# Half of a token gather issued between the router's turns and logits, and two row loads of the last norm moved

## The chip, the cores and the metric

The kernel runs on one core of a Trainium2 chip. The metric is the device time of one execution in microseconds, as the median of several runs. Three runs of the kernel before gave 711.48, 712.3 and 713.32 us, so the median is 712.3 us.

## What is computed

One decoder layer on 256 tokens of width 2048. Three token mixers (sparse attention, stick-breaking attention, forgetting attention) run on the same input, and their outputs go through one output projection and a layer norm. A mixture of experts follows, with a second layer norm:

```python
h = layer_norm(ALPHA * h + mix, ln1_g, ln1_b)
# experts: top-1 of 4 groups, then the top 2 of the 4 experts in that group
hid = silu(xt @ wg) * (xt @ wu)          # 16 experts, 2048 -> 256
y = y + (hid * gate_column) @ wd          # 256 -> 2048
h = layer_norm(ALPHA * h + y, ln2_g, ln2_b)
```

All of it is float32. The change touches the part from the first layer norm to the second.

## The kernel before, in words

**Engines and order.** TensorE's instructions run in the order in which they are written, through the whole kernel (`manual_schedule`, from line 150 on). For VectorE, ScalarE and GpSimd a planner sets most of the order up to `order.__enter__()` (line 1176); from there, within the last block of the output projection, their order is the written one too. SyncE issues the large loads in order, each as soon as its slot is free. GpSimd issues a few small loads itself (`nc.gpsimd.dma_start`).

**Tokens and halves.** The 256 tokens are two halves `t` of 128 partitions. `vt` holds the rows, `zh` and `zl` their normalised values in two parts (hi and lo) whose sum is the float32 value. The columns are 16 blocks `k` of 128.

**The router.** The last 512 columns of the output projection are finished for half 0 first, then for half 1 (`mix1`). For half 1 the row sums, the turns (`row_turn`, TensorE transposes by a matmul with `ident`), the copies of these to SBUF by ScalarE (`row_copy`), the router's logits (`row_logits`, 20 columns), the choice of experts on VectorE (`pick`, `choose`), the counting of places (a matmul with `ut`, line 1296) and the one-hots (`place`, `fill_hots`) follow each other. Half 0 has been through all of this before. `keep_warm(n)` issues n matmuls of ones into a bank that nobody reads.

**The gather.** `S0[:, t, :]` is a one-hot matrix from tokens of half t to 4 x 64 slots of the first group's experts. `gather` computes the slots' inputs with column blocks k on the partitions. A PSUM bank holds two blocks k and k + 1 of 256 slots each. For each block TensorE issues four matmuls into the bank: hi and lo of half 0, then hi and lo of half 1 (lines 908 and 909). Then ScalarE or VectorE writes the bank to `xg` with the first norm's gain and bias (`rows_out`). The first call gathers four blocks, the next four, and so on, with `gate_up_part` between.

**PSUM.** The eight banks are named: `pj` has 2, `s` has 3, `t` has 2, `o` has 1. A new tile of a name waits until the readers of that bank's last tile are done.

**The experts.** Four groups g, each with four experts in two planes `pl`. For a group, `gate_up` multiplies the slots by 16 pieces of weights of 1 MB (line 972), `hidden` and `turn` make the hidden values, the next group's gather follows, and then `down` multiplies by 8 pieces (line 1000). It does so in two rounds `c` = 0 and 2; a round has four `down`s, each into a bank of `s`, which ScalarE (L1002) and then VectorE (L1003) split into hi and lo, and two `combine`s (line 1014) that add the results into `vt` (L1015). The weight pieces go through 11 slots in turn.

**Rows of the second norm.** `lng` and `gb` hold the second norm's gain and a five-row matrix of gain and bias parts. `norm_parts(gb, h)` makes one half (1024 columns) of `gb`: a load of five rows by GpSimd (L1037) into the single buffer `raw5`, and three VectorE steps (L1038, L1039, L1040) that use the signs in `part`. In group 1 GpSimd loads `lng`, broadcasts it and makes `part` by two selects. In group 2 `norm_parts` is called for both halves, one after the other, ahead of the first round of `down`s. `gb` and `lng` are read in group 3 and by the second norm.

Of the kernel before, what the change touches and what calls it, by code (L numbers as in the profile page):

```python
# [12 lines left out]
F32 = mybir.dt.float32  # L13
# [5 lines left out]
ALU = mybir.AluOpType  # L19
# [4 lines left out]
P = 128  # L24
T = 256
# [15 lines left out]
def kernel(  # L41
# [4 lines left out]
    nc = tc.nc  # L46
    V, A, G, PE = nc.vector, nc.scalar, nc.gpsimd, nc.tensor
# [78 lines left out]
    def ps_proj():  # L126
        return psp.tile([P, 512], F32, name="pj", bufs=2)

    def ps_s():
        return psp.tile([P, 512], F32, name="s", bufs=3)  # L130

    def ps_t():
        return psp.tile([P, 512], F32, name="t", bufs=2)
# [1 line left out]
    def ps_o():  # L135
        return psp.tile([P, 512], F32, name="o", bufs=1)

    def keep_warm(n):

        w = ps_t()  # L140
        for _ in range(n):
            PE.matmul(w[:, 0:P], ones, ones, start=True, stop=True)

# [36 lines left out]
    with tc.tile_pool(name="pa", bufs=1) as pa, \  # L180
# [45 lines left out]
        start = tc.manual_schedule(engines={mybir.EngineType.DVE, mybir.EngineType.Activation})  # L226
# [17 lines left out]
        for q in range(4):  # L244
            for j, k0 in product(range(3), (q * 4, q * 4 + 2)) if q else ((0, 0), (1, 0), (2, 0), (0, 2), (1, 2), (2, 2)):
                if k0 == q * 4:
                    if q % 2 == 0:
                        parts[j] = [t.rearrange("p (a b) -> p a b", a=8) for t in parts_tile()]
                    h, l = [t[:, q % 2 * 4:q % 2 * 4 + 4, :] for t in parts[j]]
# [7 lines left out]
                h, l = parts[j]  # L257
                for k in (k0, k0 + 1):
# [10 lines left out]
                        compare_op=ALU.is_ge, fill=0.0)  # L269
        G.affine_select(out=blkm, in_=blkm, pattern=[[16, 8]], base=15, channel_multiplier=-1,  # L270
                        compare_op=ALU.is_ge, fill=0.0)
# [142 lines left out]
        def decay_turn():  # L414
            cps = ps_t()
            for t in range(2):
# [10 lines left out]
                        channel_multiplier=1, compare_op=ALU.is_ge, fill=FAR)  # L427
# [454 lines left out]
    zh, zl = by_t(hi_t), by_t(lo_t)  # L882
# [13 lines left out]
    def fill_hots(S, g, t):  # L896
        V.tensor_tensor(S[:, t, :].rearrange("p (e s) -> p e s", e=4),
                        pm[:, t, 4 * g:4 * g + 4][:, :, None].to_broadcast([P, 4, CAP]),
                        sif[:, None, 0:CAP].to_broadcast([P, 4, CAP]), op=ALU.is_equal)

    def gather(S, xg, k0=0, k1=KT, engs="AV"):

        for n, k in enumerate(range(k0, k1, 2)):
            ps = (ps_t, ps_s)[k // 2 % 2]()
            for j in range(2):
                ks = slice((k + j) * P, (k + j + 1) * P)
                for t in range(2):
                    PE.matmul(ps[:, j * T:j * T + T], zh[:, t, ks], S[:, t, :], start=t == 0, stop=False)
                    PE.matmul(ps[:, j * T:j * T + T], zl[:, t, ks], S[:, t, :], start=False, stop=t == 1)
            rows_out(ps, xg, k, engs[n % len(engs)])  # L910


# [115 lines left out]
    eps2 = pb.tile([P, 1], F32, name="eps2")  # L1028
    V.memset(eps2, EPS / (ALPHA * ALPHA))

    part = pb.tile([P, 2], F32, name="part")
    V.memset(part, 1.0)

    def norm_parts(gb, h):
        hs_ = slice(h * 1024, h * 1024 + 1024)
        raw = praw.tile([P, 1024], F32, name="raw5")[0:5, :]
        nc.gpsimd.dma_start(raw, ln2r[:, hs_])  # L1037
        V.tensor_copy(gb[0:5, hs_], raw)  # L1038
        V.tensor_scalar(raw, raw, part[0:5, 1:2], None, op0=ALU.mult)  # L1039
        V.scalar_tensor_tensor(gb[0:5, hs_], gb[0:5, hs_], part[0:5, 0:1], raw, op0=ALU.mult, op1=ALU.add)  # L1040
# [35 lines left out]
    with ExitStack() as rows:  # L1076
# [20 lines left out]
        def row_turn(t, c, js=range(4)):  # L1097
            tp = ps_t()
            for i, j in enumerate(js):
                PE.transpose(tp[:, i * P:i * P + P], vt[:, t, c * 512 + j * P:c * 512 + j * P + P], ident)  # L1100
            return tp

        def row_copy(tp, n=4):
            vT = pb2.tile([P, 4, P], F32, name="vT")
            A.activation(vT[:, 0:n, :].rearrange("p a b -> p (a b)"), tp[:, 0:n * P], AF.Copy)
            return vT

        def row_logits(vT, t, c, js=range(4)):
            for i, j in enumerate(js):
                PE.matmul(lgp[t][:, 0:20], vT[:, i, :], gw[:, c * 4 + j, 0:20],  # L1110
                          start=c + j == 0, stop=c + j == 6)
# [34 lines left out]
        def n_lo(t, c):  # L1146
            V.tensor_tensor(zl[:, t, cols[c]], vt[:, t, cols[c]], zh[:, t, cols[c]].bitcast(F32), op=ALU.subtract)
# [125 lines left out]
        row_sums(mm[1], 1, 3, range(1))  # L1273
        mix1(3, range(4), range(1, 2))
        tpa = row_turn(1, 3, range(2))
        n_lo(0, 2)
        row_sums(mm[2], 1, 3, range(1, 2))
        vTa = row_copy(tpa, 2)
        tpb = row_turn(1, 3, range(2, 4))
        row_var(1)  # L1280
        vTb = row_copy(tpb, 2)
        row_scale(1)
        row_logits(vTa, 1, 3, range(2))
        row_logits(vTb, 1, 3, range(2, 4))
        n_lo(0, 3)
        logit_mean(1)
        row_shift(1)
# [4 lines left out]
                n_norm(1, c, "A")  # L1292
        pick(1)
        choose(1)
        keep_warm(6)
        PE.matmul(pp[1][:, 0:16], ut, A2[:, 1, :], start=False, stop=True)
        keep_warm(3)
        n_lo(1, 0)
        place(1)
        fill_hots(S0, 0, 1)  # L1300
        xg = slot_rows()
        gu = ps_proj()
        n_lo(1, 1)
        n_norm(1, 2)
        gather(S0, xg, 0, 4, "A")
# [57 lines left out]
    for g in range(NG):  # L1363
        if g:
            gu = gate_up(xg, g, 0)
        gs = gates(S, g)
        C = back(S)
        hs = [hidden(gu, gs[:, 0:1])]
        S_next = one_hots(g + 1) if g + 1 < NG else None
        gu = ps_proj()  # L1370
        for kq in range(4):
            gate_up_part(gu, xg, g, 1, kq)
            if kq == 2 and g + 1 == NG:
                hT = [turn(hs[0])]
        if g + 1 < NG:
            hT = [turn(hs[0])]
        hs.append(hidden(gu, gs[:, 1:2]))
        res = None
        if g + 1 == NG:

            A.preload_act_table_set("natural_log_exp_and_others")
            res = [xs_tile() for _ in range(2)]
        if g + 1 < NG:
            S = S_next
            xg = slot_rows()
            gather(S, xg)
            hT.append(turn(hs[1]))
        if g == 1:
            nc.gpsimd.dma_start(lng[0:1, :], ln2r[0:1, :])  # L1389
            G.partition_broadcast(lng, lng[0:1, :], channels=P)  # L1390
            gb = xgp.tile([P, D], F32R, name="lnb")
            G.affine_select(out=part[:, 0:1], in_=part[:, 0:1], pattern=[[0, 1]], base=2, channel_multiplier=-1,
                            compare_op=ALU.is_ge, fill=-1.0)
            G.affine_select(out=part[:, 1:2], in_=part[:, 1:2], pattern=[[0, 1]], base=-3, channel_multiplier=1,
                            compare_op=ALU.is_ge, fill=0.0)
        if g == 2:
            norm_parts(gb, 0)
            norm_parts(gb, 1)

        for c in (0, 2):  # L1400
            parts = [slots["o"]().bitcast(F32R).rearrange("p (l i n) -> p l i n", l=2, i=2) for _ in range(2)]
            if len(hT) == 1:
                down(g, 0, 0, hT[0], parts[0])
                hT.append(turn(hs[1]))
                down(g, 1, 0, hT[0], parts[1])
                down(g, 0, 1, hT[1], parts[0])
                down(g, 1, 1, hT[1], parts[1])
            else:
                for i, pl in product(range(2), range(2)):
                    down(g, c + i, pl, hT[pl], parts[i])  # L1410
                    if g + 1 == NG:
                        gained(res, pl, i)
            for i in range(2):
                combine(c + i, C, parts[i], res)
# [102 lines left out]
```

## Time and profile before

| | |
|---|---|
| runs | 711.48, 712.3, 713.32 us (median 712.3) |
| the profiled execution's own time | 713.84 us |
| its span | 712.1 us |
| mean granted clock of TensorE | 0.981 |
| TensorE busy | 686.2 us, 96% of the span |
| VectorE busy | 418.0 us, 59% |
| ScalarE busy | 306.9 us, 43% |
| GpSimd busy | 91.7 us, 13% |

All positions below are microseconds from the start of the span of the profiled execution. The execution's own time is 1.7 us longer than its span. A matmul's shown time includes a tail that overlaps the next one, so the rate is read from starts. One matmul of float32 operands is shown as two instructions. "Idle before" in brackets is the engine's idle time just ahead of an instruction and what ended it.

### The profile page before, as it was taken

What the parts mean: (1) busy time and instruction counts of PE and PEld (TensorE: products, weight loads), DVE (VectorE), ACT (ScalarE), POOL (GpSimd) and SP (SyncE); (2) the same over time, 40 slices, a digit from 0 to 9 for tenths busy, and PEclk for the clock granted to TensorE, in tenths of its full rate; (3) what the DMA queues carried; (4) which work ended last, traced back from release to release, by engine and by line L of the source; (5) the groups of instructions that cost most, each with busy time, mean ns of one, the idle gap of its engine ahead of it and who ended that gap; (6) DMA issues with size and microseconds to landing.
All of it is one profiled execution on the core that took longest, in us unless ns stands there. A gap on an engine that the chain in (4) does not pass through costs nothing. (4 is left out here: it accounts for less than half of the span.)

```text
span 712.1 us, 11149 instructions
## 1 busy us (share of the span) xinstructions
PE 686.2 (96%) x4327; PEld 511.4 (72%) x4327; DVE 418.0 (59%) x859; ACT 306.9 (43%) x616; POOL 91.7 (13%) x128
## 2 busy tenths in 40 slices
PE   6999999999999999999999999999999999699994
PEld 6999998887789997999788889646435443443353
DVE  4768665978648976677858436474511421451186
ACT  5444555767656774567755322522201200310120
POOL 3200101454420134210020000002000000000000
PEclk9899999999999999999999999999999999989997
DMA  8964554232233355453587517489999999989923
GB/s 296 332 217 159 200 186 179 110 119 85 94 119 119 133 185 186 173 182 119 188 345 296 179 61 267 202 357 419 420 391 421 422 420 422 418 328 373 422 91 122
DMA packets 29519, 173.70 MB, mean 244 GB/s; under 512 B 4080, under 2 KB 4104, under 8 KB 10002
## 3 DMA queue, kind: packets, MB, share of 16 engines
q1 hardware_dynamic: 28192, 170.75, 62.3%
q10 hardware_dynamic: 1172, 2.12, 1.0%
q8 instruction: 36, 0.59, 0.3%
q14 instruction: 23, 0.19, 0.1%
q0 software_dynamic: 96, 0.05, 0.0%
HBM read 170.81 MB, written 2.11 MB: 243 GB/s over the span
## 5 line engine op out<-in xcount | busy, mean ns | idle before, releaser
L92 DVE TENSOR_TENSOR hl<-raw,hl 128x1024 fp32r<-128x1024 f32 x98 | 119.0, 1232 | 40.8 <-ACT hl L91 40.1
L91 ACT ACTIVATE hl<-raw 128x1024 fp32r<-128x1024 f32 x98 | 102.2, 1054 | 47.3 <-PE pj L215 14.0
L190 PE MATMUL pj<-hi_t,hl 128*128 128x256 f32 x384 | 109.3, 285 | 3.9 <-DVE hl L252 3.9
L188 PE MATMUL pj<-hi_t,hl 128*128 128x256 f32 x384 | 112.2, 292 | 0.1
L189 PE MATMUL pj<-lo_t,hl 128*128 128x256 f32 x384 | 109.1, 284 | 0.1
L190 PEld LDWEIGHTS pj<-hi_t,hl 128*128 128x128 f32 x384 | 73.8, 192 | 4.4 <-DVE hl L252 4.4
L188 PEld LDWEIGHTS pj<-hi_t,hl 128*128 128x128 f32 x384 | 73.9, 193 | 2.6 <-issue 1.7
L189 PEld LDWEIGHTS pj<-lo_t,hl 128*128 128x128 f32 x384 | 73.9, 192 | 0.6 <-DVE lo_t L256 0.4
L972 PE MATMUL pj<-raw,xs 128*64 128x512 f32 x256 | 70.7, 594 | 0.0
L972 PEld LDWEIGHTS pj<-raw,xs 128*64 128x64 f32 x256 | 21.9, 137 | 34.5 <-issue 32.3
L1002 ACT ACTIVATE ohl<-s 128x512 fp32r<-128x512 f32 x32 | 19.1, 597 | 63.2 <-PE s L1000 63.2
L972 PE MATMUL pj<-hl,xs 128*64 128x512 f32 x144 | 46.0, 594 | 0.0
L1003 DVE TENSOR_TENSOR ohl<-s,ohl 128x512 fp32r<-128x512 f32 x32 | 21.9, 688 | 32.5 <-ACT ohl L1002 32.5
L188 PE MATMUL s<-hi_t,hl 128*128 128x256 f32 x128 | 37.6, 294 | 0.5 <-ACT hl L251 0.5
L650 POOL TENSOR_SCALAR bias<-dist 128x384 f32<-128x384 f32 x16 | 23.9, 1497 | 109.7 <-DVE mx L658 60.0
L190 PE MATMUL s<-hi_t,hl 128*128 128x256 f32 x128 | 36.8, 288 | 0.2 <-DVE hl L252 0.2
L189 PE MATMUL s<-lo_t,hl 128*128 128x256 f32 x128 | 36.7, 287 | 0.0
L972 PE MATMUL pj<-xw,xs 128*64 128x512 f32 x96 | 35.6, 593 | 0.0
L1000 PE MATMUL s<-hl,hT 128*64 128x512 f32 x112 | 27.0, 627 | 7.5 <-DVE ohl L1003 7.5
L213 PE MATMUL pj<-hl,hi_t 128*128 128x512 f32 x80 | 33.3, 417 | 0.0
L215 PE MATMUL pj<-hl,hi_t 128*128 128x512 f32 x80 | 31.4, 392 | 0.0
L214 PE MATMUL pj<-hl,lo_t 128*128 128x512 f32 x80 | 31.3, 391 | 0.0
(397 smaller groups left out, 1475.1 us busy)
## 6 DMA issues: line engine op xcount, KB each, us to landing
raw<-in_egu_dram SPq DMA_DIRECT2D x32, 1024.0 KB, 7.6
raw<-in_wt_dram SPq DMA_DIRECT2D x28, 1024.0 KB, 4.8
hl<-in_egu_dram SPq DMA_DIRECT2D x18, 1024.0 KB, 10.6
hl<-in_edn_dram SPq DMA_DIRECT2D x14, 1024.0 KB, 12.7
raw<-in_edn_dram SPq DMA_DIRECT2D x13, 1024.0 KB, 13.7
raw<-in_wn_dram SPq DMA_DIRECT2D x12, 1024.0 KB, 4.8
xw<-in_egu_dram SPq DMA_DIRECT2D x12, 1024.0 KB, 10.0
raw<-in_wo_dram SPq DMA_DIRECT2D x10, 1024.0 KB, 5.0
```

What stands on the lines that cost most here:

```text
L91: A.activation(r(hi), v, AF.Copy)
L92: V.tensor_tensor(r(lo), v, r(hi).bitcast(F32), op=ALU.subtract)
L188: PE.matmul(o, h, xh[:, k, :], start=k == 0, stop=False)
L189: PE.matmul(o, h, xl[:, k, :], start=False, stop=False)
L190: PE.matmul(o, l, xh[:, k, :], start=False, stop=k == KT - 1)
L213: PE.matmul(pss[t], xh[:, k, ts], h, start=k == 0, stop=False)
L214: PE.matmul(pss[t], xl[:, k, ts], h, start=False, stop=False)
L215: PE.matmul(pss[t], xh[:, k, ts], l, start=False, stop=k == KT - 1)
L650: G.tensor_scalar(bias, dist, -SLOPE[head], None, op0=ALU.mult)
L972: PE.matmul(gu[j * 64:j * 64 + 64, :], xg[k // 8][:, k % 8, at:at + CAP], w[j][:, k4, :], start=k == 0, stop=k == KT - 1)
L1000: PE.matmul(o[j * 64:j * 64 + 64, :], hT[:, k, j * 64:j * 64 + 64], w[:, 2 * j + k, :], start=k == 0, stop=k == 1)
L1003: V.tensor_tensor(hl_[:, pl, 1, :], o, hl_[:, pl, 0, :].bitcast(F32), op=ALU.subtract)
```

## The change

- `gather` is split. `gather_bank` issues the four matmuls of one token half into a bank, and `banks` holds banks that have their first half. `start` is set on the first matmul of a bank only, and `stop` on the last.
- Four banks (column blocks 0 to 7) get the products of half 0 early: bank 0 behind the first pair of half 1's turns, bank 1 ahead of the second pair, bank 2 between the two calls of `row_logits`, bank 3 behind them. The first two come from `s`, the others from `t`. When `gather` reaches these blocks it issues the products of half 1 alone.
- `gu`, the bank of the first `gate_up`, is taken earlier, and the two calls of `keep_warm` write into it. They have 5 and 4 matmuls, where they had 6 and 3.
- The load of the rows for the second norm is a function of its own. The first half's load is issued by GpSimd in group 1 between the load of `lng` and its broadcast. In group 2 the first half's VectorE steps stay ahead of the first round of `down`s, followed by the second half's load; the second half's VectorE steps stand ahead of the second round.
- The two selects that make `part` are issued at the head of the norm stage, on a third column that holds 0.5 and -0.5; in group 1 one addition on GpSimd makes the first column from it.

```diff
--- before.py
+++ after.py
@@ -135,9 +135,9 @@
     def ps_o():
         return psp.tile([P, 512], F32, name="o", bufs=1)
 
-    def keep_warm(n):
-
-        w = ps_t()
+    def keep_warm(n, w=None):
+
+        w = ps_t() if w is None else w
         for _ in range(n):
             PE.matmul(w[:, 0:P], ones, ones, start=True, stop=True)
 
@@ -898,15 +898,23 @@
                         pm[:, t, 4 * g:4 * g + 4][:, :, None].to_broadcast([P, 4, CAP]),
                         sif[:, None, 0:CAP].to_broadcast([P, 4, CAP]), op=ALU.is_equal)
 
+    def gather_bank(S, k, ps, ts):
+        for j in range(2):
+            ks = slice((k + j) * P, (k + j + 1) * P)
+            for t in ts:
+
+                PE.matmul(ps[:, j * T:j * T + T], zh[:, t, ks], S[:, t, :], start=t + j == 0, stop=False)
+                PE.matmul(ps[:, j * T:j * T + T], zl[:, t, ks], S[:, t, :], start=False, stop=t + j == 2)
+        return ps
+
+
+    banks = []
+
     def gather(S, xg, k0=0, k1=KT, engs="AV"):
 
         for n, k in enumerate(range(k0, k1, 2)):
-            ps = (ps_t, ps_s)[k // 2 % 2]()
-            for j in range(2):
-                ks = slice((k + j) * P, (k + j + 1) * P)
-                for t in range(2):
-                    PE.matmul(ps[:, j * T:j * T + T], zh[:, t, ks], S[:, t, :], start=t == 0, stop=False)
-                    PE.matmul(ps[:, j * T:j * T + T], zl[:, t, ks], S[:, t, :], start=False, stop=t == 1)
+            ps = banks.pop(0) if banks else gather_bank(S, k, (ps_t, ps_s)[k // 2 % 2](), range(1))
+            gather_bank(S, k, ps, range(1, 2))
             rows_out(ps, xg, k, engs[n % len(engs)])
 
 
@@ -1028,13 +1036,21 @@
     eps2 = pb.tile([P, 1], F32, name="eps2")
     V.memset(eps2, EPS / (ALPHA * ALPHA))
 
-    part = pb.tile([P, 2], F32, name="part")
+    part = pb.tile([P, 3], F32, name="part")
     V.memset(part, 1.0)
-
-    def norm_parts(gb, h):
+    V.memset(part[:, 2:3], 0.5)
+    G.affine_select(out=part[:, 2:3], in_=part[:, 2:3], pattern=[[0, 1]], base=2, channel_multiplier=-1,
+                    compare_op=ALU.is_ge, fill=-0.5)
+    G.affine_select(out=part[:, 1:2], in_=part[:, 1:2], pattern=[[0, 1]], base=-3, channel_multiplier=1,
+                    compare_op=ALU.is_ge, fill=0.0)
+
+    def norm_load(h):
+        raw = praw.tile([P, 1024], F32, name="raw5")[0:5, :]
+        nc.gpsimd.dma_start(raw, ln2r[:, h * 1024:h * 1024 + 1024])
+        return raw
+
+    def norm_parts(gb, raw, h):
         hs_ = slice(h * 1024, h * 1024 + 1024)
-        raw = praw.tile([P, 1024], F32, name="raw5")[0:5, :]
-        nc.gpsimd.dma_start(raw, ln2r[:, hs_])
         V.tensor_copy(gb[0:5, hs_], raw)
         V.tensor_scalar(raw, raw, part[0:5, 1:2], None, op0=ALU.mult)
         V.scalar_tensor_tensor(gb[0:5, hs_], gb[0:5, hs_], part[0:5, 0:1], raw, op0=ALU.mult, op1=ALU.add)
@@ -1273,15 +1289,20 @@
         row_sums(mm[1], 1, 3, range(1))
         mix1(3, range(4), range(1, 2))
         tpa = row_turn(1, 3, range(2))
+        banks.append(gather_bank(S0, 0, ps_s(), range(1)))
         n_lo(0, 2)
         row_sums(mm[2], 1, 3, range(1, 2))
         vTa = row_copy(tpa, 2)
+        banks.append(gather_bank(S0, 2, ps_s(), range(1)))
         tpb = row_turn(1, 3, range(2, 4))
         row_var(1)
         vTb = row_copy(tpb, 2)
         row_scale(1)
         row_logits(vTa, 1, 3, range(2))
+        banks.append(gather_bank(S0, 4, ps_t(), range(1)))
         row_logits(vTb, 1, 3, range(2, 4))
+        banks.append(gather_bank(S0, 6, ps_t(), range(1)))
+        gu = ps_proj()
         n_lo(0, 3)
         logit_mean(1)
         row_shift(1)
@@ -1292,14 +1313,13 @@
                 n_norm(1, c, "A")
         pick(1)
         choose(1)
-        keep_warm(6)
+        keep_warm(5, gu)
         PE.matmul(pp[1][:, 0:16], ut, A2[:, 1, :], start=False, stop=True)
-        keep_warm(3)
+        keep_warm(4, gu)
         n_lo(1, 0)
         place(1)
         fill_hots(S0, 0, 1)
         xg = slot_rows()
-        gu = ps_proj()
         n_lo(1, 1)
         n_norm(1, 2)
         gather(S0, xg, 0, 4, "A")
@@ -1387,17 +1407,18 @@
             hT.append(turn(hs[1]))
         if g == 1:
             nc.gpsimd.dma_start(lng[0:1, :], ln2r[0:1, :])
+            raw5 = norm_load(0)
             G.partition_broadcast(lng, lng[0:1, :], channels=P)
+
+            G.tensor_tensor(part[:, 0:1], part[:, 2:3], part[:, 2:3], op=ALU.add)
             gb = xgp.tile([P, D], F32R, name="lnb")
-            G.affine_select(out=part[:, 0:1], in_=part[:, 0:1], pattern=[[0, 1]], base=2, channel_multiplier=-1,
-                            compare_op=ALU.is_ge, fill=-1.0)
-            G.affine_select(out=part[:, 1:2], in_=part[:, 1:2], pattern=[[0, 1]], base=-3, channel_multiplier=1,
-                            compare_op=ALU.is_ge, fill=0.0)
         if g == 2:
-            norm_parts(gb, 0)
-            norm_parts(gb, 1)
+            norm_parts(gb, raw5, 0)
+            raw5 = norm_load(1)
 
         for c in (0, 2):
+            if g == 2 and c:
+                norm_parts(gb, raw5, 1)
             parts = [slots["o"]().bitcast(F32R).rearrange("p (l i n) -> p l i n", l=2, i=2) for _ in range(2)]
             if len(hT) == 1:
                 down(g, 0, 0, hT[0], parts[0])
```

## Rows read from the trace of the kernel before

**Rows 1.** The page's first part: busy us, share of the span, instructions by engine.

```profile
PE 686.2 (96%) x4327; PEld 511.4 (72%) x4327; DVE 418.0 (59%) x859; ACT 306.9 (43%) x616; POOL 91.7 (13%) x128
```

**Rows 2.** The chain that ended last: start us, us, what.

```profile
615.85 5.21 DMA raw<-in_ln2r_dram
```

**Rows 3.** Timeline of TensorE, 610:632: start, us, engine, line, out<-in, [idle before].

```profile
611.60 5.37 PE L1000 MATMUL s<-hl,hT 128*64 128x512 f32 x24
624.50 3.48 PE L1000 MATMUL s<-hl,hT 128*64 128x512 f32 x8 [7.53 <-DVE ohl L1003]
...
631.77 0.65 PE L1000 MATMUL s<-raw,hT 128*64 128x512 f32 x2
```

**Rows 4.** Timeline of VectorE, 610:633.

```profile
612.73 0.67 DVE L1038 CAST lnb<-raw 5x1024 fp32r<-5x1024 f32 x1
...
614.28 1.27 DVE L1040 SCALAR_TENSOR_TENSOR lnb<-lnb,part,raw 5x1024 fp32r<-5x1024 f32 x1
621.08 0.68 DVE L1038 CAST lnb<-raw 5x1024 fp32r<-5x1024 f32 x1 [5.52 <-DMA raw<-in_ln2r_dram]
...
623.77 1.87 DVE L1003 TENSOR_TENSOR ohl<-s,ohl 128x512 fp32r<-128x512 f32 x3
```

**Rows 5.** Timeline of TensorE, 443.2:454.5.

```profile
444.41 0.44 PE L1100 MATMUL t<-ident,full 128*128 128x128 f32 x2 [0.68 <-DVE full L1093]
...
445.88 0.62 PE L1110 MATMUL o<-gw,vT 128*128 128x20 f32 x4 [0.67 <-ACT vT L1105]
...
449.06 1.43 PE L142 MATMUL t<-ones 128*128 128x128 f32 x6
450.24 0.36 PE L908 MATMUL t<-S,hi_t 128*128 128x256 f32 x1
...
454.07 0.65 PE L972 MATMUL pj<-ohl,xs 128*64 128x512 f32 x2
```

**Rows 6.** Timeline of VectorE, 449:450.

```profile
449.69 0.42 DVE L897 TENSOR_TENSOR S<-pm,sif 128x256 fp32r<-128x256 f32 x1
```

**Rows 7.** Busy us by stretch: PE, PEld, DVE, ACT, POOL, clock, DMA share, GB/s.

```profile
443.30:446.70 3.40, 2.06 (x17) 1.72 (x17) 3.08 (x12) 1.80 (x6) 0.00 (x0) 1.00 1.01 417
446.80:450.10 3.30, 3.17 (x17) 2.91 (x16) 2.99 (x15) 3.23 (x6) 0.00 (x0) 0.50 1.02 429
```

**Rows 8.** Timeline of TensorE, 552:567 (group 1).

```profile
553.33 3.65 PE L1000 MATMUL s<-xw,hT 128*64 128x512 f32 x16
...
564.20 3.22 PE L1000 MATMUL s<-hl,hT 128*64 128x512 f32 x14
```

**Rows 9.** Timeline of VectorE, 552:567 (group 1).

```profile
564.31 0.69 DVE L1015 TENSOR_TENSOR full<-o,full 128x512 f32<-128x512 f32 x1 [0.21 <-PE o L1014]
566.81 0.69 DVE L1003 TENSOR_TENSOR ohl<-s,ohl 128x512 fp32r<-128x512 f32 x1 [1.81 <-ACT ohl L1002]
```

**Rows 10.** Busy us by stretches of 10 us.

```profile
630.00:640.00 10.00, 10.00 (x46) 4.42 (x45) 4.61 (x7) 2.39 (x4) 0.00 (x0) 1.00 0.75 271
640.00:650.00 10.00, 10.00 (x48) 4.40 (x49) 2.90 (x5) 0.00 (x0) 0.00 (x0) 1.00 0.84 334
650.00:660.00 10.00, 10.00 (x60) 3.63 (x58) 0.80 (x3) 0.87 (x2) 0.00 (x0) 1.00 1.01 423
```

**Rows 11.** DMA issues in 661:661.5: engine, count, KB, us to landing.

```profile
raw<-in_edn_dram SPq DMA_DIRECT2D x1, 1024.0 KB, 11.5
```

**Rows 12.** Timeline of TensorE, 670:692 (group 3).

```profile
675.66 3.60 PE L1000 MATMUL s<-raw,hT 128*64 128x512 f32 x16
```

**Rows 13.** DMA issues in 481:490.

```profile
raw<-in_ln2r_dram POOLq DMA_DIRECT2D x1, 20.0 KB, 5.5
```

**Rows 14.** Timelines of GpSimd and VectorE, 340:366.

```profile
345.43 0.89 POOL L598 TENSOR_TENSOR ssq<-ssq,sq 128x256 f32<-128x256 f32 x1 [7.49 <-ACT sq L597]
...
365.69 0.06 DVE L1032 MEMSET part<- 128x2 f32 x1
```

## The prediction

> **What bounds the kernel now.** I read the page's busy table first: TensorE is busy 96% of the span [rows 1], so time can only come out of stretches where it stands idle or runs slow, or out of work that it need not do there. The chain of waits came next. In the expert stage, where the chain runs along TensorE for long stretches, it shows one piece of another kind: a transfer of the second norm's rows, 5.21 us, at 615.85 [rows 2]. TensorE's timeline around it shows a pause of 7.53 us before the instruction at 624.50, put down to VectorE's L1003, and that group of 8 instructions takes 3.48 us where 24 took 5.37 us just before [rows 3]. VectorE's timeline says why: its second L1038 starts at 621.08 and was held 5.52 us by that very transfer, and L1003, which frees the PSUM banks of `down`, stands behind it in VectorE's order [rows 4]. The buffer `raw5` is single, so the second load may start only when the first half's L1040 has read it, at 614.28 + 1.27 = 615.55.
>
> The stretch that the change is named after is the router, 443 to 454 us. There TensorE waits 0.68 us for VectorE and 0.67 us for ScalarE, multiplies ones with ones as a filler, and then issues the gather [rows 5]. The second token half's one-hots, which half of that gather needs, are written by VectorE from 449.69 for 0.42 us [rows 6]. The chain of small VectorE steps that ends there sets when the second half can begin; the first half's products wait for nothing in it.
>
> **The change part by part.** *The gather's first half.* 32 matmuls stand between 450.24 and 454.07 [rows 5]: 3.83 us, 0.12 us each. 16 of them (four banks, two columns of 128, hi and lo) move ahead. What is left is 16 x 0.12 = 1.9 us, and the first of these needs the one-hots that end at 449.69 + 0.42 = 450.11. Before, the gather began at 450.24, so it can't begin much earlier; the gain is the 1.9 us by which it is shorter.
>
> What the moved products cost where they now stand: a bank is 4 x 0.12 = 0.47 us. Banks 0 and 1 go in front of the second pair of turns, into the 0.68 us wait before 444.41. Together they are 0.94 us, but a turn's shown time has a tail that overlaps what follows (matmuls of 0.36 us start 0.12 us apart), so I expect about 0.05 us of delay. What waits for these turns is ScalarE's copy and then the second logits at 445.88, which had 0.67 us of waiting; bank 2's 0.47 us goes into that. Bank 3 stands behind the logits, where only filler follows. If the cover were gone, all four would cost 4 x 0.47 = 1.9 us and the part would give nothing. PSUM: two banks come from `s`, two from `t`. The `t` banks were last read by ScalarE's copies of the turns, and for the second of these copies the logits at 445.88 have waited anyway. The filler moves to a `pj` bank whose row sums came before the turns at 444.41. Filler calls go from 6 + 3 to 5 + 4. The last 6 instructions of filler took from 449.06 to 450.24, 0.2 us each, at the half clock of [rows 7]; with 8 the filler ends near 449.9 at full clock and near 450.6 at half, against a gather that can begin at about 450.2. So this part lies between 1.5 and 1.9 us; I take 1.9.
>
> *The second norm's rows.* The first load goes on GpSimd's queue ahead of the broadcast, in group 1. The broadcast waits there for a transfer of its own, so an issue ahead of it costs nothing, and the first half's VectorE work in group 2 goes on as now, at 612.73 [rows 4]. The second load keeps its trigger (615.55) and, I expect, its 5.2 us, so it lands at about 621.1. But VectorE now goes on to L1003 and asks for it only behind the combines of the first two column blocks.
>
> Group 1 runs the same code without norm work and gives the undisturbed length: from its first `down` at 553.33 to the first `down` of the next two blocks at 564.20 are 10.87 us [rows 8]. In group 2 the same distance is 631.77 - 611.60 = 20.17 us [rows 3]. The difference, 9.30 us, is the pause of 7.53 us plus what the slower instructions behind it lose. It goes if nothing is late in its place.
>
> What could be late: VectorE reaches the second half's norm work 0.80 us after the next `down`s start (its last combine in group 1 ends at 564.31 + 0.69, against 564.20) [rows 8, 9], so at 611.60 + 10.87 + 0.80 = 623.27. The load has landed 2.2 us before. The three steps take from 621.08 to about 623.8, some 2.7 us [rows 4], so to 626.0. L1003 would otherwise start 2.61 us behind the `down`s [rows 9], at 625.08, so it comes 0.95 us late and frees the first bank at 626.7. TensorE wants that bank for its fourth `down`, three times 1.75 us after 622.47, at 627.7 (24 instructions of [rows 3] are three `down`s). One microsecond in hand: no wait. The two small selects of `part` go to the head of the norm stage and leave one addition on GpSimd, behind the broadcast and over 100 us ahead of its reader; I cost these at nothing.
>
> *Weights in the last group.* TensorE reaches group 3 9.30 us earlier against its loads (the 1.9 us of the router shift both, since slots come free that much earlier). The DMA engines run at 423 GB/s in 650:660, but at 271 and 334 GB/s in 630:640 and 640:650 [rows 10]: slots held by the paused TensorE left the queue short. That is (152 + 89) GB/s x 10 us = 2.4 MB, or 5.7 us at 423 GB/s, which comes back when slots are released on time. The tightest place is the fourth `down` of group 3: its weights are issued at 661.08 and land after 11.5 us, at 672.6 [rows 11], and it starts half-way into the 16 instructions of 675.66, at about 677.4 [rows 12]. That is 4.8 us in hand; after the change 4.8 - 9.3 + 5.7 = 1.2 us. I take no wait.
>
> **Sum:** 1.9 + 9.3 = 11.2 us. The profiled execution took 713.84 us with a span of 712.1; it would become 702.6. The median shown is 712.3, 1.5 us under that execution, so the median should be 701.1 us.
>
> **Rivals.** *A, the forecast: 701.1 us.*
>
> [...]
>
> *C, the second load is held up by VectorE.* Before, it ran while VectorE stood idle waiting for it; now VectorE is at work. If it could not start until VectorE pauses, at 623.27, it would land at 628.5, the norm work would end at 631.2, the bank be free at 631.9: TensorE waits 4.2 us from 627.7. The gain is 7.0 us: 705.3. Against it: the first load, issued in 481:490 with VectorE at work on group 0, landed after 5.5 us, against 5.2 [rows 2, 13]. [...]
>
> *D, the weights bound group 3.* If the queue won back none of its 5.7 us, TensorE would wait 9.3 - 4.8 = 4.5 us there: gain 6.7, time 705.6. Against it: the release of slots is TensorE's own progress, which comes earlier by the same change.
>
> *E, slower.* Place: GpSimd's in-order queue before the norm stage. The two selects read a memset on VectorE that belongs with the one at 365.69. The planner orders GpSimd's work there. If it puts the selects ahead of the sum of squares that ran at 345.43 [rows 14], that sum waits for the memset, at least 20.3 us, and TensorE with it, as the output projection needs its result: 712.3 - 11.2 + 20.3 = 721.4. It decides at that place: behind the last of these sums the selects cost nothing, for what follows on GpSimd is wanted only by the experts' norm much later. Against it: a planner that goes by readiness has no reason to.
>
> **How the numbers follow.** Chances: A 0.60; B with its twin 0.20; C 0.07; D 0.08; E 0.03; something between D and E, with no net change, 0.02. The low end of the range is A less the 0.9 us by which the shown runs spread, and the 0.4 us of the best case for the filler: 699.8. The high end is D at its full price, rounded up: 705.7. About 0.3% (2 us) is what a measurement of this kernel can tell from no change. A to D are all at least 6.7 us faster, so faster 0.95, same 0.02, slower 0.03.
>
> **What would show it.** In the changed profile TensorE's wait for L1003 at about 615 us is gone, the next `down`s start 10.9 us behind the first ones in group 2 as in group 1, and the two norm triples of VectorE lie some 10 us apart with no wait for the transfer in front of the second. The DMA rate stays near 420 GB/s through the 630s. In the router 8 gather instructions stand ahead of the second turns, and the gather's rest takes 1.9 us from about 450.2, with the clock at 1.0 throughout. B shows as a clock of 0.5 there, C as a wait of the second L1038, D as TensorE waiting for a weight transfer in group 3. The prediction is wrong if the pause merely moves to the next place where VectorE meets the load, or if TensorE's end moves by less than 9 us.

## The result, and the profile after

The changed kernel takes 695.86 us (median of 4 runs, 695.26 to 696.12), beside 712.81 us of the kernel before on the same chip (4 runs, 711.48 to 714.43): a ratio of 0.976, 95% interval 0.9738 to 0.9782. The forecast was 701.1 us with a range down to 699.8, so the time lies 5.2 us under the forecast and 3.9 us under the range. By the two medians the change saved 16.95 us where 11.2 were forecast. The profiled execution took 695.73 us with a span of 693.9.

The page, its first part (busy us, share of the span, instructions), the granted clock and the DMA rate in 40 slices:

```profile
PE 679.9 (98%) x4327; PEld 507.4 (73%) x4327; DVE 421.7 (61%) x860; ACT 306.9 (44%) x616; POOL 93.7 (13%) x129
...
PEclk9999999999999999999999999999999999999997
...
GB/s 308 370 242 167 200 192 182 115 70 122 66 118 122 155 179 183 162 181 144 176 313 356 188 60 190 296 284 420 420 389 422 422 422 422 420 415 423 418 154 125
```

TensorE is busy 6.3 us less than in [rows 1], and its share rose from 96% to 98%. From the 31st slice to the 38th (520 to 659 us) the rate lies between 415 and 423 GB/s; in [rows 10] it had fallen to 271 and 334 in two stretches of that time.

I matched the TensorE instructions of the two traces and followed how much earlier each one starts. Three steps make up the 18.2 us by which the span is shorter (the medians differ by 16.95; the profiled execution of before, 713.84 us, was 1.0 us above its median here):

- by 23 us from the start: 7.0 us. It stays at 7.0 to 7.2 up to the router. Nothing in the prediction speaks of this place.
- from the count matmul behind the filler to the first gate_up (454.07 in [rows 5], now 445.13): from 7.18 to 8.94, so 1.76 us.
- in group 2, across the second norm's rows: from 8.94 to 18.23, so 9.3 us.

**The two steps that were foreseen.** TensorE around the second norm's rows, 595 to 632 us (start us, us, engine, line, operation):

```profile
602.66 7.09 PE L1008 MATMUL s<-hl,hT 128*64 128x512 f32 x32
...
613.55 7.09 PE L1008 MATMUL s<-raw,hT 128*64 128x512 f32 x32
```

The two rounds of four `down`s stand 10.89 us apart, as in group 1 (10.87, [rows 8]), against 20.17 in [rows 3]; no idle time is shown ahead of them. VectorE there:

```profile
605.34 1.27 DVE L1056 SCALAR_TENSOR_TENSOR lnb<-lnb,part,raw 5x1024 fp32r<-5x1024 f32 x1
...
614.26 0.67 DVE L1054 CAST lnb<-raw 5x1024 fp32r<-5x1024 f32 x1
...
615.75 1.27 DVE L1056 SCALAR_TENSOR_TENSOR lnb<-lnb,part,raw 5x1024 fp32r<-5x1024 f32 x1
616.95 0.67 DVE L1011 TENSOR_TENSOR ohl<-s,ohl 128x512 fp32r<-128x512 f32 x1
```

The first half's last step ends at 606.61, and the second half's begins at 614.26, 7.65 us later, with no wait for a transfer; in [rows 4] it waited 5.52 us. L1011 (the line that was L1003) follows at 616.95 with no idle time in front of it. The issues of 604 to 616 us (count, KB, us to landing):

```profile
raw<-in_ln2r_dram POOLq DMA_DIRECT2D x1, 20.0 KB, 5.5
```

The second load landed 5.5 us after its issue, while VectorE was at work. So rival C didn't occur. Rival D didn't either: no wait of TensorE for a weight transfer is left in the expert stage.

The router, TensorE from 439 to 450 us, then the windows (busy us of PE, PEld, DVE, ACT, POOL; clock; DMA share; GB/s):

```profile
439.72 1.27 PE L142 MATMUL pj<-ones 128*128 128x128 f32 x10
441.85 0.17 PE L1317 MATMUL s<-A,ut 128*128 128x16 bf16 x1 [0.85 <-DVE A L1270]
441.87 1.14 PE L142 MATMUL pj<-ones 128*128 128x128 f32 x8
443.08 0.36 PE L906 MATMUL s<-S,hi_t 128*128 128x256 f32 x1
...
445.13 3.65 PE L980 MATMUL pj<-ohl,xs 128*64 128x512 f32 x16
```

```profile
439.80:443.10 3.30, 2.38 (x21) 2.04 (x19) 2.99 (x14) 3.26 (x5) 0.00 (x0) 1.00 1.01 427
443.10:446.50 3.40, 3.40 (x24) 2.41 (x26) 2.74 (x5) 3.16 (x7) 0.00 (x0) 1.00 0.92 388
```

The moved half is gone from the path: 16 gather matmuls between 443.08 and 445.13 where [rows 5] has 32 in 3.83 us. The first window stands for the one of 446.80:450.10 in [rows 7], where the clock was 0.50, and the second for the gather behind it. The clock is 1.00 in both, although TensorE paused for 0.85 us ahead of the count; rival B, a clock of 0.5 there, didn't occur. From the first of the 8 fillers behind the count to the gather are 1.21 us (443.08 less 441.87), where the 6 of [rows 5] took 1.18.

**The step that was not.** GpSimd in the kernel before, its first 20 us (idle time before it and what ended it in brackets; "issue" is time in which it waited for nothing that the profile shows):

```profile
0.93 0.32 POOL L282 MEMSET ks<- 128x256 f32 x1
12.25 0.48 POOL masks.py:199 TENSOR_SCALAR_AFFINE_SELECT ident<-ident 128x128 f32<-128x128 f32 x1 [11.00 <-issue]
...
17.06 0.10 POOL L567 MEMSET halfm<- 128x2 f32 x1
```

VectorE there:

```profile
17.16 0.48 DVE L445 TENSOR_SCALAR bc<-dc 128x32 f32<-128x32 f32 x3 [4.58 <-POOL halfm L567]
17.56 0.68 DVE L252 TENSOR_TENSOR hl<-raw,hl 128x512 fp32r<-128x512 f32 x1
```

And TensorE:

```profile
14.29 0.28 PE L189 MATMUL pj<-lo_t,hl 128*128 128x256 f32 x1
18.29 0.58 PE L190 MATMUL pj<-hi_t,hl 128*128 128x256 f32 x1 [3.72 <-DVE hl L252]
18.67 0.42 PE L188 MATMUL pj<-hi_t,hl 128*128 128x256 f32 x1
```

These are to be read as one chain. GpSimd idles 11.00 us ahead of its first select, so its whole setup ends late. VectorE's L445 builds small rows from that setup; it starts at 17.16, after 4.58 us of idle time. L252, a split of the projection's weights, stands behind L445 in VectorE's order and starts 0.40 us behind it, at 17.56. TensorE waits 3.72 us for it, and then runs at half clock (0.51 over 16.6 to 23.5): matmuls of 0.42 us instead of 0.28. GpSimd and VectorE in the changed kernel:

```profile
0.93 0.32 POOL L282 MEMSET ks<- 128x256 f32 x1
1.54 0.29 POOL masks.py:199 TENSOR_SCALAR_AFFINE_SELECT ident<-ident 128x128 f32<-128x128 f32 x1 [0.29 <-POOL ks L282]
...
7.08 0.09 POOL L567 MEMSET halfm<- 128x2 f32 x1
```

```profile
11.52 0.35 DVE L445 TENSOR_SCALAR bc<-dc 128x32 f32<-128x32 f32 x3
11.78 0.69 DVE L252 TENSOR_TENSOR hl<-raw,hl 128x512 fp32r<-128x512 f32 x1
```

The first select starts at 1.54, L445 at 11.52, and L252 0.26 us behind it. The stretch 16.6 to 23.5, TensorE's busy time first and the clock after the five engines, of the kernel before:

```profile
16.60:23.50 6.90, 5.21 (x24) 5.21 (x25) 6.34 (x25) 2.67 (x6) 1.62 (x8) 0.51 1.02 360
```

and of the changed kernel:

```profile
16.60:23.50 6.90, 6.90 (x60) 6.90 (x59) 4.86 (x7) 3.50 (x6) 0.00 (x0) 1.00 1.00 368
```

24 matmuls became 60. Pause (3.72 us) and half clock (24 matmuls that start 0.213 us apart instead of 0.12: 2.2 us) give 5.9 of the 7.0 us. 0.9 us is there at 14 us already, ahead of the pause. A second trace of the changed kernel (the last experiment) doesn't have it and is 6.1 us ahead of before at 25 us, where this one is 7.2 us ahead: of the 7.0, about 1 us is luck, a difference between executions of one kernel.

No line of the head was changed. But GpSimd also has entries that these timelines leave out, in pairs called MODIFY_POOL_CONFIG. In the kernel before there are two pairs, ahead of the first select and of the first norm's broadcasts; in the changed kernel a third stands ahead of the addition. In the compiled program each pair is one request to reload a numbered library: number 0 at the head, 1 ahead of the broadcasts, and 0 again ahead of the addition. The pair at the head (count, shortest, median and longest in ns, first and last start in us), before:

```profile
masks.py:199 POOLq MODIFY_POOL_CONFIG  x2: 11/11/11, 1.3 to 1.3; - x2
```

and the three pairs of the changed kernel:

```profile
masks.py:199 POOLq MODIFY_POOL_CONFIG  x2: 8/10/13, 1.4 to 1.5; - x2
...
L879 POOLq MODIFY_POOL_CONFIG  x2: 11/11/11, 359.3 to 359.4; - x2
...
L1413 POOLq MODIFY_POOL_CONFIG  x2: 123/123/123, 481.2 to 481.3; - x2
```

GpSimd after, at the broadcasts and the addition:

```profile
369.53 4.25 POOL L879 PARTITION_BROADCAST lng<-lng  x1 [10.15 <-issue]
...
479.03 2.29 POOL L1411 PARTITION_BROADCAST lng<-lng  x1 [5.20 <-DMA lng<-in_ln2r_dram]
490.63 0.18 POOL L1413 TENSOR_TENSOR part<-part 128x1 f32<-128x1 f32 x1 [9.31 <-issue]
```

10.15 us ahead of the first norm's broadcast, 9.31 us ahead of the addition, neither with a wait that the profile shows; the broadcast at 479.03 has no such pair and waits only for its transfer. **Theory:** these pairs load code for GpSimd ("code" is my reading of the request's name). The broadcast needs another library than the addition; each change costs the idle time behind its pair (9.31, 10.15 and 11.00 us in these two traces), what is loaded stays from one execution to the next, and a request for what is already there costs next to nothing (at the head of the changed kernel the pair starts at 1.4 us and the select at 1.54). The kernel before ends with the broadcast's library, so every execution opens with a load, on the path. The addition changes the library back in group 1, where nobody waits, and the next execution opens without a load. **Rivals:** the moved selects or the moved loads freed the head; or the two executions differ there by chance.

### The profile page after: what moved, and what is told of

Read it like the earlier page. It is cut to its first block, busy times and chain, and to the rows that moved or that the text cites. A ratio compares the mean times of both kernels' runs of the same rounds, so it can differ in the third digit from the quotient of the medians.

```text
span 693.9 us, 11152 instructions
## 1 busy us (share of the span) xinstructions
PE 679.9 (98%) x4327; PEld 507.4 (73%) x4327; DVE 421.7 (61%) x860; ACT 306.9 (44%) x616; POOL 93.7 (13%) x129
## 4 chain that ended last, share of the span: by engine, by line
PE 90%; DVE 4%; POOL 2%; issue 1%; ACT 1%; DMA 1%; SPq 0%; DVEq 0%; POOLq 0%
PE pj L980 16%; PE s L1008 8%; PE pj L188 6%; PE pj L189 6%; PE pj L190 6%; PE pj L175 2%; PE t L1022 2%; PE pj L177 2%; PE pj L176 2%; PE pj L213 2%; PE s L188 2%; PE s L190 2%; PE s L189 2%; PE pj L215 2%; PE t L619 2%; PE pj L214 2%
## 5 line engine op out<-in xcount | busy, mean ns | idle before, releaser
L1011 DVE TENSOR_TENSOR ohl<-s,ohl 128x512 fp32r<-128x512 f32 x32 | 22.0, 689 | 28.8 <-ACT ohl L1010 28.8
L660 ACT ACTIVATE bg<-bg,mx 128x128 f32<-128x128 f32 (+1 forms) x64 | 28.2, 443 | 0.5 <-DVE mx L658 0.2
```

What stands on the lines that cost most here:

```text
L660: A.activation(pr[:, br, ks_], pr[:, br, ks_], AF.Exp, bias=mx[:, half, t, br:br + 1], scale=-1.0, accum_out=sm8[:, half, t, br:br + 1])
```

## The experiments

**Take the addition out.** The changed kernel with `part` as before:

```diff
-    part = pb.tile([P, 3], F32, name="part")
+    part = pb.tile([P, 2], F32, name="part")
     V.memset(part, 1.0)
-    V.memset(part[:, 2:3], 0.5)
-    G.affine_select(out=part[:, 2:3], in_=part[:, 2:3], pattern=[[0, 1]], base=2, channel_multiplier=-1,
-                    compare_op=ALU.is_ge, fill=-0.5)
-    G.affine_select(out=part[:, 1:2], in_=part[:, 1:2], pattern=[[0, 1]], base=-3, channel_multiplier=1,
-                    compare_op=ALU.is_ge, fill=0.0)
...
-            G.tensor_tensor(part[:, 0:1], part[:, 2:3], part[:, 2:3], op=ALU.add)
             gb = xgp.tile([P, D], F32R, name="lnb")
+            G.affine_select(out=part[:, 0:1], in_=part[:, 0:1], pattern=[[0, 1]], base=2, channel_multiplier=-1,
+                            compare_op=ALU.is_ge, fill=-1.0)
+            G.affine_select(out=part[:, 1:2], in_=part[:, 1:2], pattern=[[0, 1]], base=-3, channel_multiplier=1,
+                            compare_op=ALU.is_ge, fill=0.0)
```

> The changed kernel with `part` as it was before: two columns, both selects behind the broadcast in group 1, no addition. Theory (GpSimd keeps its code from one execution to the next; the addition, last but for a DMA, brings back the code that the kernel's first select needs): without it the 11 us of idle time before GpSimd's first select come back at the head, VectorE's L445 starts at about 17 us instead of 11.5, TensorE pauses for about 3.7 us at 14.5 and runs at half clock to about 23: 695.9 + 7.0 = 702.9 us (702.4 to 703.6). Rival (the 7 us at the head came with the moved loads, the moved selects or from another state of the chip): 695.9 us, first select at 1.5 us.

Measured: 701.24 us (699.87 to 702.22), ratio to the kernel before 0.9817 (0.9789 to 0.9845). GpSimd and TensorE at the head:

```profile
11.23 0.30 POOL masks.py:199 TENSOR_SCALAR_AFFINE_SELECT ident<-ident 128x128 f32<-128x128 f32 x1 [9.99 <-issue]
```

```profile
17.54 0.58 PE L190 MATMUL pj<-hi_t,hl 128*128 128x256 f32 x1 [3.49 <-DVE hl L252]
```

The load is back, and with it the pause. The time is under the 702.4 to 703.6 expected, where I had put the load at 7.0 us. In this trace the idle time is 9.99 us and the pause 3.49, and TensorE ends the head 0.5 us ahead of the trace of before. From there the lead grows to 2.3 us behind the router and to 11.6 us behind the norm's rows: the forecast's own two steps, alone. This is the kernel that my forecast of 701.1 us describes.

**Put only the addition in.** The kernel before, with one line more behind the selects and a third column in `part`:

```diff
+            G.tensor_tensor(part[:, 2:3], part[:, 2:3], part[:, 2:3], op=ALU.add)
```

> The kernel before and one GpSimd addition more, on a spare column of `part`, behind the two selects of group 1; nothing else of the change. Theory (resident code): the addition shows 9 to 10 us of idle time before it, off the path, and the next execution's first select starts at 1.5 us: 712.8 - 7.0 = 705.8 us (705.2 to 706.4), with the two other savings of the change (1.8 and 9.3 us) absent. Rival: one addition more changes nothing, 712.8 us, 11 us idle before the first select.

Measured: 707.95 us (707.19 to 708.51), ratio 0.9915 (0.9883 to 0.9946); the kernel before took 713.82 beside it. GpSimd:

```profile
1.54 0.29 POOL masks.py:199 TENSOR_SCALAR_AFFINE_SELECT ident<-ident 128x128 f32<-128x128 f32 x1 [0.30 <-POOL ks L282]
...
494.69 0.18 POOL L1396 TENSOR_TENSOR part<-part 128x1 f32<-128x1 f32 x1 [10.30 <-issue]
```

An addition of 0.18 us, of which nothing is used, made the kernel 5.9 us faster. It costs an idle time of 10.30 us where GpSimd has nothing else to do, and the first select moves to 1.54. The two selects just ahead of it ran directly behind the broadcast (at 483.96 and 484.10, behind its 2.29 us from 481.81), without such a pair.

**The same instructions, another order.** The changed kernel with its addition one line earlier:

```diff
+            G.tensor_tensor(part[:, 0:1], part[:, 2:3], part[:, 2:3], op=ALU.add)
             G.partition_broadcast(lng, lng[0:1, :], channels=P)
-
-            G.tensor_tensor(part[:, 0:1], part[:, 2:3], part[:, 2:3], op=ALU.add)
```

> The changed kernel with its addition one line earlier, ahead of the broadcast of group 1 instead of behind it: the same instructions, another order. Theory (the last kind of code decides): two idle times of 9 to 10 us in group 1, one before the addition and one before the broadcast, neither on the path; the program ends with the broadcast's code, so the head has its 11 us again: 702.9 us (702.4 to 703.6). Rival 1 (an addition anywhere in group 1, or the selects' new place, frees the head): 695.9 us. Rival 2 (the two loads of code themselves hold up the second norm's rows): over 703.6 us, with a wait at the second norm.

Measured: 701.04 us (700.07 to 701.9), ratio 0.9817 (0.9789 to 0.9846). GpSimd, then TensorE:

```profile
10.74 0.28 POOL masks.py:199 TENSOR_SCALAR_AFFINE_SELECT ident<-ident 128x128 f32<-128x128 f32 x1 [9.49 <-issue]
...
489.43 0.18 POOL L1411 TENSOR_TENSOR part<-part 128x1 f32<-128x1 f32 x1 [10.49 <-issue]
499.41 2.30 POOL L1412 PARTITION_BROADCAST lng<-lng  x1 [9.80 <-issue]
```

```profile
17.03 0.53 PE L190 MATMUL pj<-hi_t,hl 128*128 128x256 f32 x1 [3.49 <-DVE hl L252]
```

Two loads in group 1 instead of one (10.49 and 9.80 us), both hidden, and a third at the head of the next execution (9.49 us). The head's own instructions are the same in both orders, so what differs there can only come from what the execution before left behind. That settles it against the moved selects and loads, which stand here as in the changed kernel. The effect on the time is 4.6 to 5.2 us against the two medians of the changed kernel (695.86 and 696.43, measured apart from it), not the 7 expected; against the run without the addition (701.24, measured beside it) there is no difference.

**Leave the load, take away who waits for it.** The kernel before with L445's 16 multiplications on GpSimd:

```diff
-                    V.tensor_scalar(bc[:, :, s, :], dc, -SLOPE[head], NEG, op0=ALU.mult, op1=ALU.max)
+                    G.tensor_scalar(bc[:, :, s, :], dc, -SLOPE[head], NEG, op0=ALU.mult, op1=ALU.max)
```

> The kernel before with the 16 small multiplications of L445 (bc<-dc) on GpSimd instead of VectorE; nothing of the change. Theory (the late code costs time only because these multiplications stand in VectorE's queue ahead of the splits that TensorE waits for): GpSimd still idles 11 us before its first select, but VectorE's L252 no longer waits behind L445, TensorE has no pause at 14.5 us: 712.8 - 7.0 = 705.8 us (705 to 706.5). Rival (the head is held by another thing that GpSimd makes, or by the clock alone): 711 to 712.8 us.

Measured: 708.14 us (707.7 to 711.32), ratio 0.9924 (0.9897 to 0.9951), so 5.7 us under the 713.82, where 7.0 were expected. GpSimd, VectorE, and TensorE's window (busy, clock behind the engines):

```profile
13.59 0.33 POOL masks.py:199 TENSOR_SCALAR_AFFINE_SELECT ident<-ident 128x128 f32<-128x128 f32 x1 [12.34 <-issue]
```

```profile
13.07 2.05 DVE L252 TENSOR_TENSOR hl<-raw,hl 128x512 fp32r<-128x512 f32 x3
```

```profile
15.00:24.00 9.00, 9.00 (x77) 9.00 (x77) 7.14 (x11) 5.51 (x10) 8.55 (x26) 1.00 1.03 362
```

GpSimd idles even longer, 12.34 us, but L252 starts at 13.07, TensorE has no pause at 14.5 us, and from 15 to 24 us it is busy all the time at a clock of 1.00. So the load costs its time through VectorE's order. (This profiled execution, 710.22 us, is 2.1 us above its median: it waited 1.02 us for ScalarE until 8.91 us, and its matmuls start 0.21 us apart from there to 13.9 us and 0.12 us apart behind that.) By their medians this cure and the addition's are worth nearly the same.

**Each of the foreseen parts alone.** The kernel before with the norm's loads as in the change (`norm_load` split off, the first call in group 1, the second half's work behind the first two column blocks), selects and router as before:

```diff
-    def norm_parts(gb, h):
+    def norm_load(h):
+        raw = praw.tile([P, 1024], F32, name="raw5")[0:5, :]
+        nc.gpsimd.dma_start(raw, ln2r[:, h * 1024:h * 1024 + 1024])
+        return raw
+
+    def norm_parts(gb, raw, h):
         hs_ = slice(h * 1024, h * 1024 + 1024)
-        raw = praw.tile([P, 1024], F32, name="raw5")[0:5, :]
-        nc.gpsimd.dma_start(raw, ln2r[:, hs_])
...
             nc.gpsimd.dma_start(lng[0:1, :], ln2r[0:1, :])
+            raw5 = norm_load(0)
...
-            norm_parts(gb, 0)
-            norm_parts(gb, 1)
+            norm_parts(gb, raw5, 0)
+            raw5 = norm_load(1)
 
         for c in (0, 2):
+            if g == 2 and c:
+                norm_parts(gb, raw5, 1)
```

> The kernel before with the two loads of the second norm's rows moved as in the change; the selects of `part` stay in group 1 behind the broadcast, no addition, no banks in the router. Theory: 9.3 us less at the second norm and nothing else, TensorE's 7.53 us wait gone and its clock not lowered there, GpSimd's 11 us at the head still there: ratio to the kernel before 0.987, some 703.5 us where that takes 712.8. Rival (the moved loads free the head too, by other work on GpSimd's queue): some 696.5 us, first select at 1.5 us.

Measured: 702.83 us (702.38 to 703.87), ratio 0.9861 (0.984 to 0.9882), with the kernel before at 712.85. TensorE and GpSimd:

```profile
609.52 7.09 PE L1000 MATMUL s<-hl,hT 128*64 128x512 f32 x32
...
620.41 7.09 PE L1000 MATMUL s<-raw,hT 128*64 128x512 f32 x32
```

```profile
12.18 0.48 POOL masks.py:199 TENSOR_SCALAR_AFFINE_SELECT ident<-ident 128x128 f32<-128x128 f32 x1 [10.93 <-issue]
```

The rounds of `down`s stand 10.89 us apart, and the head has its load, so the moved loads alone don't free it. The kernel before with the gather banks and the filler's bank as in the change (`gather_bank` and `keep_warm` too, not shown), nothing else:

```diff
...
+        banks.append(gather_bank(S0, 0, ps_s(), range(1)))
...
+        banks.append(gather_bank(S0, 2, ps_s(), range(1)))
...
+        banks.append(gather_bank(S0, 4, ps_t(), range(1)))
...
+        banks.append(gather_bank(S0, 6, ps_t(), range(1)))
+        gu = ps_proj()
...
-        keep_warm(6)
+        keep_warm(5, gu)
...
-        keep_warm(3)
+        keep_warm(4, gu)
...
-        gu = ps_proj()
```

> The kernel before with the four gather banks' first halves moved among the turns and logits, and keep_warm into the gate bank; the norm loads, the selects and the addition as before. Theory: 1.8 us less between the router and the first gate_up, nothing elsewhere: ratio 0.9975, some 711 us where the kernel before takes 712.8. Rival (the moved products lower TensorE's clock in the router or hold up its logits): 712.8 us or more.

Measured: 711.01 us (709.06 to 712.06, 12 runs), ratio 0.9968 (0.9953 to 0.9983): 1.8 us, as expected; the second norm's wait was there, 7.6 us.

These two traces show what the load's price hangs on. The idle times are 10.93 and 11.74 us, but TensorE's pause for L252 is only 1.46 and 1.65 us: it had waited for ScalarE until 8.27 and 9.36 us (0.96 and 2.06 us), its matmuls started 0.21 us apart behind that, to 14.5 and 15.2 us, instead of 0.12, and so it came to L252 late by itself.

**The changed kernel again, and with both cures.** On the chip of the two parts, the changed kernel as it is, and with L445 on GpSimd as above:

> The changed kernel as it is, as a yardstick on the chip of this call. Every theory: ratio to the kernel before 0.976, some 696 us; GpSimd's first select at 1.5 us.

> The changed kernel with the 16 small multiplications of L445 on GpSimd, as in the run with the rows on GpSimd. Theory (the two cures act on the same 7 us): with the code resident there is no pause left to take away, the same time as the changed kernel of this call within 1 us, some 695 to 696 us. Rival (VectorE's 16 multiplications cost head time of their own, 16 x 0.09 = 1.4 us): 694.5 us. Second rival (they cost GpSimd's later setup): over 697 us.

Measured: 696.43 us (695.67 to 696.79), ratio 0.9764; with both 696.18 us (695.71 to 696.31), ratio 0.9761 (0.9744 to 0.9779). The second cure finds nothing left to cure, so the two act on the same time. It does not beat the changed kernel by anything that can be measured.

The three edits alone give 10.0, 1.8 and 5.9 us, 17.7 together; the whole gave 16.4 beside the first two. The difference is within what the runs of the kernel before spread (711.2 to 716.99 there).

## Why the prediction was wrong

**The step that failed** is the last one under the second norm's rows: "The two small selects of `part` go to the head of the norm stage and leave one addition on GpSimd, behind the broadcast and over 100 us ahead of its reader; I cost these at nothing." As a cost in its own place that holds: 9.31 us of load and 0.18 us of work, all hidden. As a term of the sum it was worth some 5 to 6 us of gain: 5.9 alone; 4.8 when it was taken out of the change (701.24 less 696.43, on two chips); 4.6 to 5.2 by the order. With 11.2 us for the rest that is 15.8 to 17.1 us, and 16.95 were measured. The 7.0 us of the first two traces are the largest difference that any pair of traces shows: at 25 us from the start, the five executions with the load ahead of VectorE's L445 stand 0 to 2.3 us ahead of the trace of before, and the four without it 6.1 to 7.2 us.

What led to it: I priced an instruction by its duration, and looked for what it might hold up behind it. I did not ask what state of the engine it leaves behind. The trace of before had the hint: 11 us of idle GpSimd ended by "issue" ahead of its first select, and a TensorE pause of 3.72 us for VectorE in the same stretch. I had begun my reading at the long pause and the router and taken the head for something that the change does not touch. Behind the MODIFY_POOL_CONFIG pairs the traces show no instruction, only idle time of 8.8 to 12.3 us. That what is loaded stays from one execution to the next is what the addition's two orders show: 9.49 us of idle time ahead of the first select where the broadcast came last, 0.29 us where the addition did.

**The rest, by its steps.** The gather's half: 1.9 us forecast, 1.76 in the trace, 1.8 alone; the filler at full clock (1.00 in 439.8 to 443.1) took the whole place that I left for it. The norm's rows: 9.3 forecast, 9.3 in the trace, 10.0 alone (9.3 in that run's own trace, from 2.07 to 11.36 us of lead; the rest is its head). VectorE reached the second half 7.65 us behind the end of the first, forecast 7.72 (623.27 less 615.55). The second load took 5.5 us to land, forecast 5.2. Weights: no wait, and the rate stayed up as forecast. B, C and D didn't occur. Rival E was decided on its harmless side: the selects ran at 359.06, behind the last sum of squares (349.05 + 0.74). The sum of 11.2 us, a ratio of 0.984 to the 712.3 shown, lies inside the interval of the change without its addition (0.9789 to 0.9845).

**What stays open.** Why a load takes 8.8 us in one place and 12.3 in another was not tried. What passes in it isn't seen: from 1.3 to 12.2 us of the kernel before, only packets of the queue that carries the program's own loads are recorded. So that it is code was not shown and rests on the name of the request alone; that it hangs on what the execution before left is shown. Which kinds of operation share a library was only seen where it occurred: selects ran behind the broadcast without a load (at 483.96 in the run with the addition alone, with no idle time in front), the addition did not (9.31 to 10.95 us), so which operation of the setup wants the load at the head is open. What an execution finds behind another kernel, no run here shows.

## What to carry to other kernels

Look at the first microseconds of a trace as at any other stretch: the 9.49 to 12.34 us of idle GpSimd that ended in "issue" here, behind a pair of MODIFY_POOL_CONFIG, came and went with the last GpSimd work of the program, and whether such a stretch is on the path is told by who stands behind its first results in the other engines' order. In these runs, of one kernel again and again, the last GpSimd work decided what the next execution found. Where a trace shows the same, end with the kind of work that the program begins with, or make the switch where GpSimd is idle. And when an edit swaps one operation of GpSimd for another kind, price the switch (8.80 to 10.95 us here), in both directions, and not the instruction alone.

## What the runs showed of the hardware

- Where the program's last request was for the broadcast's library, the first select of the profiled execution waited 9.49 to 12.34 us (six of them); where it was for the addition's, 0.29 to 0.30 us (four).
- A switch between the broadcast's and the addition's library cost 8.80 to 10.15 us ahead of the first norm's broadcasts (the four executions whose profile names no other wait there), 9.80 us ahead of the broadcast of group 1 behind the addition, and 9.31 to 10.95 us ahead of the addition, with nothing shown but a pair of MODIFY_POOL_CONFIG at its start (two of 0.12 us in the changed kernel).
- A pause of TensorE of 3.72 us, ended at 18.29, came with a mean granted clock of 0.51 over 16.6 to 23.5, though TensorE was at work again for 5.2 us of it; without the pause the clock was 1.00 there. Behind the pauses of 1.46 and 1.65 us in the traces of the two parts alone the matmuls started 0.12 us apart, behind one of 3.49 us with the addition first 0.21 us apart.
